# The opening of a two-layer transformer trunk: rows turned ahead of the modulation, its sums split over two engines, weights laid out in slabs by the host, and a written order on three engines

## The chip, the cores and the metric

The kernel runs on one core of one Trainium2 chip. The metric is device time in microseconds (us) of one launch; the median of three runs before the change is 1437.43 us (1436.27 to 1440.77).

In the rows, PE is TensorE (matmuls and transposes), PEld its weight loads, DVE VectorE, ACT ScalarE, POOL GpSimd; SPq is the queue on which SyncE issues most DMAs.

## The reference, cut to what matters

512 rows of 1024 go through two layers. The opening is the first block's modulated norm and its projection to queries and keys:

```python
cond = silu(c)
mod = cond @ ada_w[0] + ada_b[0]                 # (1, 6 * 1024)
sh1, sc1, g1, sh2, sc2, g2 = split(mod, 6)
h = rms_norm(x, norm_mix[0]) * (1 + sc1) + sh1   # (512, 1024)
q, k, v = split(h @ a_w_in, 3)                   # a_w_in: (1024, 3072)
q, k = rms_norm of each head of 64
```

Then come attention with a position bias, the output projection, a squared-ReLU MLP, a second layer with spatial gating in place of attention, and its MLP.

## The kernel before

Every float32 matmul is made of three passes over rounded halves, high by high, high by low and low by high (`mm3`). So each weight tile is split after it is loaded: ScalarE casts the high half, VectorE subtracts for the low half (`wload`, lines 402 and 403; `wload_half`, 854 and 855). Memory is a pool of 49 slots (`SL`), PSUM 8 banks (`bank`).

The opening cuts the 1024 input columns into four chunks of 256. For a chunk, `stage_load` loads eight slab rows of `ada_w` for shift and scale (each 128 x 512, shift and scale side by side) and lets VectorE add them, each times its element of `cs`, into one running sum (line 209). For chunk 0 the shift half goes another way: `shift_first` lets TensorE make the sums, one column of 128 at a time. `stage_mod` sums the partitions by four matmuls of one column, closes shift and scale (lines 893 to 896), turns the normed rows of the chunk's two blocks of 128 by transposes (`turn`, line 902), modulates each block on ScalarE (line 911), and splits it (916, 917). `stage_q0` and `stage_q1` are the chunk's share of the query columns 0 to 511 and 512 to 767: 24 matmuls of 512 columns and 24 of 256. After chunk 3 comes the K block: `gemm_tok(h, k_w, t, ps)` for four tiles of rows, 96 matmuls of 512 columns, which needs all eight blocks of `h`. Its banks are two free ones and then those of the queries, which come free when `qk_norm` (lines 982 to 988) has normed and copied them out. Then the attention heads begin, with the rest of the projection as filler.

Instructions are placed on each engine by a scheduler that works before the run, and each engine then keeps its order. Some stretches are written in order for TensorE by `in_order()`; the opening isn't. `bg` puts the sums of later modulations behind the instruction in `mark`.

Of the kernel before, what the change touches and what calls it, by code (L numbers as in the profile page):

```python
# [52 lines left out]
def trunk_kernel(  # L53
# [37 lines left out]
    def bank():  # L91
        return PS.get([P, 512], F32)
# [41 lines left out]
    ps, i = bank()  # L134
    T.transpose(ps[:, 0:P], vecs, ident)
    V.tensor_copy(vecT, ps[:, 0:P])
    T.transpose(ps[:, P:P + 2], qk2, ident[0:2, 0:2])
    V.tensor_scalar(qkg[:, 0:1], ps[:, P:P + 1], -0.5 * HD ** -0.5, None, ALU.mult)
    V.tensor_scalar(qkg[:, 1:2], ps[:, P + 1:P + 2], -0.5, None, ALU.mult)
    PS.free(i)  # L140
# [38 lines left out]


# [4 lines left out]
    def ada_acc(l, ms, c0, n, box):  # L185
# [5 lines left out]
        def load(k0):  # L191
            box[k0] = raw, done = raw_tile([P, kl, nm * n])
            src = ada_w[l].rearrange("(p k) (m j) -> p k m j", p=P, m=6)[:, k0:k0 + kl, ms[0]:ms[-1] + 1, c0:c0 + n]
            for k in range(kl if nm > 1 else 0):
                SP.dma_start(raw[:, k, :].rearrange("p (m j) -> p m j", m=nm), src[:, k])
            if nm == 1:
                SP.dma_start(raw, src[:, :, 0, :])
# [91 lines left out]
    region = []  # L289

    def in_order():
        region.append(tc.manual_schedule(engines={mybir.EngineType.PE}))
        region[-1].__enter__()
# [99 lines left out]
    def wload(src, nk, k0=0, engs=(V,)):  # L393
# [3 lines left out]
        for k in range(k0, k0 + nk, kp):  # L397
# [7 lines left out]
            w += [(hi[:, o, :], lo[:, o, :]) for o in range(kp)]  # L405
            ids += [i, j]
# [431 lines left out]
    rows = [norm_rows(t, V) for t in range(NT)]  # L838
    SL.free(*xid)
    first = [bank() for t in range(NT)]  # L840
    second = [bank() for _ in range(NT // 2)]
    first_ids = []
    zeros, zi = SL.get([P, 512], F32R)
    G.memset(f32(zeros), 0.0)
    for ps, _ in second:
        mm(ps, ones, zeros, True, False)

    def wload_half(src, k0, nk, eng):

        raw, done = raw_tile([P, nk, 256])  # L850
        loaded[0] = SP.dma_start(raw, src[k0 * P:(k0 + nk) * P, :].rearrange("(k p) n -> p k n", p=P))
        hi, i = SL.get([P, nk, 256], F32R)
        lo, j = SL.get([P, nk, 256], F32R)
        A.copy(hi, raw)
        eng.tensor_tensor(lo, raw, f32(hi), ALU.subtract)
        done()
        first_ids.extend([i, j])
        return [(hi[:, o, :], lo[:, o, :]) for o in range(nk)]

    def shift_first(n):  # L860

        nk, kl = n // P, D // n
        ps, pi = bank()
        mm(ps[:, 0:nk], ones, zeros[:, 0:nk], True, False)
        modT[0, 0] = cp.tile([P, KD], F32, name="mod00")
        for k0 in range(0, KD, kl):
            raw, done = raw_tile([P, kl, n])
            SP.dma_start(raw, ada_w[0].rearrange("(p k) j -> p k j", p=P)[:, k0:k0 + kl, 0:n])
            for k in range(kl):
                for j in range(nk):  # L870
                    mm(
                        ps[:, j:j + 1], raw[:, k, j * P:(j + 1) * P], cs[:, k0 + k:k0 + k + 1],
                        False, k0 + k == KD - 1 and j == nk - 1,
                    )
            done()
        V.tensor_tensor(modT[0, 0][:, 0:nk], ps[:, 0:nk], vecT[:, 0:nk], ALU.add)
        PS.free(pi)

    def mod_columns(c0, n, accs):

        k0, nk = c0 // P, n // P
        ps, pi = bank()
        for i, (m, acc) in enumerate(accs):
            if (0, m) not in modT:
                modT[0, m] = cp.tile([P, KD], F32, name=f"mod0{m}")
            r = modT[0, m][:, k0:k0 + nk]
            for j in range(nk):
                o = i * nk + j
                mm(ps[:, o:o + 1], acc[:, j * P:(j + 1) * P], f32(ones)[:, 0:1], True, True)
            col = m * KD + k0  # L890
            src = ps[:, i * nk:(i + 1) * nk]
            if m == 0:
                V.tensor_tensor(r, src, vecT[:, col:col + nk], ALU.add)
            else:
                V.scalar_tensor_tensor(r, src, 1.0, vecT[:, col:col + nk], ALU.add, ALU.add)
                V.tensor_tensor(r, r, vecT[:, 96 + k0:96 + k0 + nk], ALU.mult)
        PS.free(pi)

    def turn(k):
        ps, pi = bank()  # L900
        for t in range(NT):
            T.transpose(ps[:, t * P:(t + 1) * P], rows[t][0][:, k * P:(k + 1) * P], ident)
        return ps, pi

    split = [None]

    def modulate(turned, k0):
        for o, (ps, pi) in enumerate(turned):
            tt = tp.tile([P, 512], F32, tag="tt", name="tt")
            k = k0 + o  # L910
            A.activation(
                tt, ps, AF.Identity, bias=modT[0, 0][:, k:k + 1], scale=modT[0, 1][:, k:k + 1],
            )
            PS.free(pi)
            hi, lo = h[k]
            split[0] = A.copy(hi, tt)
            mark[0] = V.tensor_tensor(lo, tt, f32(hi), ALU.subtract)

    cw, nk = 256, 2
    state = {}  # L920

    def stage_load(ci):
        c0, k0 = ci * cw, ci * nk
        box = {}
        if ci == 0:
            shift_first(cw)
        for load, use in ada_acc(0, (1,) if ci == 0 else (0, 1), c0, cw, box):
            load()
            use()
        w, ids = wload(a_w_in[0][:, 0:512], nk, k0)  # L930
        first_ids.extend(ids)
        w2 = wload_half(a_w_in[0][:, 512:768], k0, nk, V)
        state[ci] = box, w, w2

    def stage_mod(ci):
        c0, k0 = ci * cw, ci * nk
        box = state[ci][0]
        turned = [turn(k0)]
        ms = (1,) if ci == 0 else (0, 1)
        mod_columns(c0, cw, [(m, box["acc"][:, i * cw:(i + 1) * cw]) for i, m in enumerate(ms)])  # L940
        SL.free(box["id"])
        turned += [turn(k0 + 1)]
        modulate(turned, k0)

    def stage_q0(ci):
        for t in range(NT):
            gemm_tok(h, state[ci][1], t, first[t][0], ci * nk, KD - 1)

    def stage_q1(ci):
        k0 = ci * nk  # L950
        for t in range(NT):
            ps = second[t // 2][0][:, t % 2 * 256:t % 2 * 256 + 256]
            gemm_tok(h, state[ci][2], t, ps, k0, KD - 1 + (t + 1) % 2, False)

    stage_load(0)
    stage_mod(0)
    for ci in range(1, 4):
        stage_load(ci)
        stage_q0(ci - 1)
        stage_mod(ci)  # L960
        stage_q1(ci - 1)
    stage_q0(3)
    stage_q1(3)
    SL.free(zi, *[i for _, i in rows])
    for l, m in ((0, 2), (0, 4), (0, 3), (0, 5), (1, 1), (1, 0), (1, 2), (1, 4), (1, 3), (1, 5)):
        bgq.extend(ada_mod(l, m))

    qk = {}
# [541 lines left out]
```

## Time and profile before

| | us |
|---|---|
| median of three runs | 1437.43 |
| the profiled execution, its own time | 1437.91 |
| its span, first to last instruction | 1436.1 |
| TensorE busy in the span | 1391.4 |
| VectorE, ScalarE busy | 1020.0, 709.1 |
| mean granted TensorE clock, of full speed | 0.988 |

The span is 1.8 us shorter than the time of the same execution. A busy TensorE is not one at its peak: at half the clock it is as busy.

### The profile page before, as it was taken

To read this page: it belongs to the slowest core of one execution; us is meant where nothing else is said; L and a number is where in the kernel's file an instruction comes from. 1 tells how busy PE (TensorE), PEld (TensorE's weight loads), DVE (VectorE), ACT (ScalarE), POOL (GpSimd) and SP (SyncE) were. 2 spreads that over 40 slices of the span, in tenths; PEclk is the share of its full clock that TensorE was granted. 3 is DMA by queue.
4 is the path that set the end of the run, shared out by engine and by line. 5 is a ranking of instruction groups with operands and counts; after the bars stand their busy time and mean duration, and the time that the engine had idled before them with its cause. 6 is when DMAs were issued, how large, how long until landed. Compare 5 with 4: busy or idle time off the path is not lost.

```text
span 1436.1 us, 18871 instructions
## 1 busy us (share of the span) xinstructions
PE 1391.4 (97%) x7186; PEld 1191.1 (83%) x7186; DVE 1020.0 (71%) x1493; ACT 709.1 (49%) x1228; POOL 10.0 (1%) x34
## 2 busy tenths in 40 slices
PE   6989889899999999999999999999999999999998
PEld 5879879779988888888888888788889988888887
DVE  6577899767577877786996754667677366776882
ACT  4426677655454543555677542233346455453630
POOL 0000000000000000000000000000000000000000
PEclk9999999999999999999999999999999999999999
DMA  9736654556236263167133343345337226152141
GB/s 335 242 107 188 195 175 126 184 205 235 73 118 219 75 220 103 38 223 275 66 118 105 123 128 111 114 140 183 103 132 264 76 72 196 54 162 88 30 161 59
DMA packets 95459, 208.93 MB, mean 145 GB/s; under 512 B 7808, under 2 KB 25608, under 8 KB 95368
## 3 DMA queue, kind: packets, MB, share of 16 engines
q1 hardware_dynamic: 95184, 207.66, 44.5%
q8 instruction: 56, 0.92, 0.3%
q14 instruction: 35, 0.29, 0.1%
q10 hardware_dynamic: 184, 0.07, 0.0%
HBM read 190.92 MB, written 8.39 MB: 139 GB/s over the span
## 4 chain that ended last, share of the span: by engine, by line
PE 77%; DMA 2%; DVE 1%; ACT 1%; issue 0%; SPq 0%; DVEq 0%; ACTq 0%
PE p L95 76%; DMA s<-in_ffn_w 1%; DVE s L403 1%; PE p L1421 1%; PE p L329 1%; DMA s<-in_b_w_in 0%; ACT s L480 0%; DMA s<-in_b_w_out 0%; PE p L222 0%; PE p L380 0%; DVE s L481 0%; ACT s L402 0%; ACT tt L333 0%; DVE s L1119 0%; DVE s L1143 0%
## 5 line engine op out<-in xcount | busy, mean ns | idle before, releaser
L95 PE MATMUL p<-s,s 128*128 128x512 f32 (+2 forms) x6568 | 1333.0, 363 | 19.9 <-DVE s L988 4.1
L95 PEld LDWEIGHTS p<-s,s 128*128 128x128 f32 x6568 | 1117.5, 191 | 208.4 <-ACT ry L151 4.5
L481 DVE TENSOR_TENSOR s<-s,s 128x1024 fp32r<-128x1024 f32 x234 | 280.3, 1219 | 113.0 <-ACT s L480 53.7
L480 ACT CAST s<-s 128x1024 fp32r<-128x1024 f32 x234 | 241.6, 1051 | 174.5 <-PE p L95 109.4
L403 DVE TENSOR_TENSOR s<-s,s 128x1024 fp32r<-128x1024 f32 x102 | 123.3, 1221 | 70.5 <-ACT s L402 59.3
L402 ACT CAST s<-s 128x1024 fp32r<-128x1024 f32 x102 | 106.3, 1050 | 114.4 <-DMA s<-in_b_w_in 27.8
L209 DVE SCALAR_TENSOR_TENSOR s<-s,cs,s 128x1024 f32<-128x1024 f32 (+2 forms) x98 | 108.6, 1109 | 12.9 <-DMA s<-in_ada_w 11.8
L628 DVE TENSOR_TENSOR s<-s,s 128x1024 f32<-128x1024 f32 x64 | 77.3, 1219 | 34.1 <-DMA s<-in_ffn_w 30.9
L736 ACT ACTIVATE r<-p 128x512 f32<-128x512 f32 x64 | 38.1, 595 | 116.7 <-PE p L95 116.6
L514 DVE TENSOR_TENSOR s<-p,s 128x512 f32<-128x512 f32 x104 | 70.3, 684 | 34.6 <-PE p L95 33.4
L742 ACT ACTIVATE s<-r 128x256 f32<-128x256 f32 (+1 forms) x112 | 44.9, 443 | 1.2
L421 DVE TENSOR_TENSOR tr<-p,s 128x512 f32<-128x512 f32 (+1 forms) x33 | 21.9, 670 | 30.3 <-PE p L95 30.0
L318 ACT ACTIVATE s<-s 128x512 f32<-128x512 f32 x32 | 20.2, 632 | 37.8 <-DVE s L422 34.8
L1081 ACT ACTIVATE s<-s,nm 128x384 f32<-128x384 f32 (+3 forms) x64 | 35.7, 559 | 6.3 <-DVE nm L1076 4.6
L1402 ACT CAST s<-s 128x512 fp32r<-128x512 f32 x24 | 14.5, 620 | 44.2 <-DVE s L1400 25.6
L1427 DVE TENSOR_TENSOR s<-p,s 128x256 fp32r<-128x256 f32 x48 | 19.8, 416 | 21.8 <-ACT s L1426 21.7
L1398 ACT ACTIVATE s<-p 128x512 f32<-128x512 f32 x24 | 14.3, 598 | 40.8 <-PE p L95 40.6
L1076 DVE CUSTOM_DVE_ANT_0 s<-p,s 128x384 f32<-128x384 f32 (+3 forms) x64 | 28.8, 484 | 7.6 <-PE p L95 6.1
L527 DVE TENSOR_TENSOR s<-s,s 128x1024 f32<-128x1024 f32 x28 | 33.5, 1217 | 1.0 <-PE p L95 0.9
L1119 DVE TENSOR_TENSOR s<-p,s 128x512 fp32r<-128x512 f32 (+3 forms) x64 | 29.2, 481 | 0.9 <-ACT s L1118 0.8
L1114 PE MATMUL p<-ident,s 128*128 128x128 f32 x160 | 24.0, 276 | 5.8 <-ACT sq L1195 3.2
L1426 ACT CAST s<-p 128x256 fp32r<-128x256 f32 x48 | 17.5, 372 | 24.2 <-PE p L1421 17.6
(129 smaller groups left out, 680.4 us busy)
## 6 DMA issues: line engine op xcount, KB each, us to landing
s<-in_ffn_w SPq DMA_DIRECT2D x128, 512.0 KB, 4.6
s<-in_ada_w SPq DMA_DIRECT2D x84, 512.0 KB, 4.5
s<-in_b_w_in SPq DMA_DIRECT2D x48, 512.0 KB, 4.7
s<-in_b_w_out SPq DMA_DIRECT2D x24, 512.0 KB, 4.8
s<-in_a_w_in SPq DMA_DIRECT2D x22, 512.0 KB, 6.5
s<-s SPq DMA_DIRECT2D x64, 128.0 KB, 2.5
s<-in_ada_w SPq DMA_DIRECT2D x24, 256.0 KB, 6.6
s<-in_x SPq DMA_DIRECT2D x8, 512.0 KB, 5.3
```

Source lines behind the costliest of these rows:

```text
L95: T.matmul(ps, lhsT, rhs, start=start, stop=stop, skip_group_check=more)
L209: V.scalar_tensor_tensor(acc, r, ck, acc, ALU.mult, ALU.add)
L402: A.copy(hi, raw)
L403: engs[len(ids) // 2 % len(engs)].tensor_tensor(lo, raw, f32(hi), ALU.subtract)
L480: A.copy(self.hi, raw)
L481: mark[0] = V.tensor_tensor(self.lo, raw, f32(self.hi), ALU.subtract)
L514: V.tensor_tensor(dst, ps, dst, ALU.add)
L527: V.tensor_tensor(self.ab[d][0], self.ab[a][0], self.ab[b][0], o)
L628: V.tensor_tensor(x[0], y_[0], z[0], ALU.subtract)
L736: A.activation(r, ps, AF.Relu)
L742: A.activation(d, v, AF.Square)
L1081: A.activation(pt[it], pt[it], AF.Exp, bias=nm[:, it:it + 1], scale=-1.0, accum_out=sm[:, it:it + 1])
```

## The change

All rows of `x` are normed and turned ahead of the modulation; blocks that wait are copied from their banks into slots (`keep_turned`). The half of the squares of a row goes to VectorE. A chunk's eight slab rows are shared: TensorE takes three of chunk 0 and one of chunk 1 as columns (`column_of`), VectorE the others (`add_part`). The host lays out `ada_w` and `a_w_in` so that a load is one contiguous run of 4 KB (one of 2 KB) per partition. TensorE, VectorE and ScalarE keep the written order from the start of the opening to `any_order()`. 20 matmuls of zeros run first. The mark for the background sums is set on the last query norm.

```diff
 def ada_acc(l, ms, c0, n, box): ... def load(k0):
-            for k in range(kl if nm > 1 else 0):
-                SP.dma_start(raw[:, k, :].rearrange("p (m j) -> p m j", m=nm), src[:, k])
...
+                src = flat(ada_w, (c0 // n * P * KD + k0) * 512, [[KD * 512, P], [1, kl * 512]])
+                SP.dma_start(raw.rearrange("p k n -> p (k n)"), src)
...
+    def wload_slabs(src, offset, count, n, engs=(V,)):
...
+            loaded[0] = SP.dma_start(
+                raw.rearrange("p k n -> p (k n)"), flat(src, offset + s * P * 1024, [[1024, P], [1, 1024]])
+            )
...
-    rows = [norm_rows(t, V) for t in range(NT)]
...
+    in_order(ENG.PE, ENG.DVE, ENG.Activation)
+    u = st.tile([P, 1], F32, tag="ry1", name="ry")
+    A.activation(u, f32(ones)[:, 0:1], AF.Abs_reciprocal_sqrt)
...
+    for i in range(20):
+        mm(sums[0][0], ones, zeros, True, True)
...
+    def norm_sums(t):
...
+        A.activation(nt[:, 0:512], xt[t][:, 0:512], AF.Square, scale=D ** -0.5, accum_out=ss[:, 0:1])
+        V.tensor_tensor_reduce(
+            out=nt[:, 512:D], in0=xt[t][:, 512:D], in1=xt[t][:, 512:D], scale=1.0 / D, scalar=EPS,
+            op0=ALU.mult, op1=ALU.add, accum_out=ss[:, 1:2],
+        )
...
+    def norm_scale(t):
...
+        nt, c = rows[t][0], (D, 0, D, 512)[t]
+        if c:
+            V.tensor_scalar(nt[:, 0:c], xt[t][:, 0:c], u, None, ALU.mult)
+        if c < D:
+            A.activation(nt[:, c:D], xt[t][:, c:D], AF.Copy, scale=u)
...
+    def keep_turned(k):
...
+        A.copy(nT[k // 2][0][:, k % 2, :], ps)
+        PS.free(pi)
...
+    def column(ci, src, right, stop=False):
+        for j in range(4):
+            mm(sums[ci][0][:, j:j + 1], src[:, j * P:(j + 1) * P], right, False, stop and j == 3)
...
+    def add_part(ci, k):
...
+            V.tensor_scalar(box["acc"], r, cs[:, k:k + 1], None, ALU.mult)
+        else:
+            V.scalar_tensor_tensor(box["acc"], r, cs[:, k:k + 1], box["acc"], ALU.mult, ALU.add)
...
+    def end_columns(ci):
+        box = accs[ci][0]
+        column(ci, box["acc"], f32(ones)[:, 0:1], True)
...
+    def mod_close(ci):
...
+        V.scalar_tensor_tensor(sc, ps[:, NC:2 * NC], 1.0, vecT[:, KD + k0:KD + k0 + NC], ALU.add, ALU.add)
+        V.scalar_tensor_tensor(sc, sc, -0.5, vecT[:, 96 + k0:96 + k0 + NC], ALU.mult, ALU.mult)
+        V.tensor_tensor(sh, ps[:, 0:NC], vecT[:, k0:k0 + NC], ALU.add)
...
+    def stage_q(ci, n):
+        for o, (wh, wl) in enumerate(chunks[ci][0][n]):
+            k = ci * NC + o
+            ah, al = h[k]
+            for i, (l, r) in enumerate(((ah, wh), (ah, wl), (al, wh))):
+                for t in range(NT):
...
+    V.tensor_copy(vecT, vps[:, 0:P])
...
+    for k in (2, 3, 4, 5, 7):
+        add_part(0, k)
+    column_of(0, 6)
+    w_load(0)
+    ada_load(1)
+    keep_turned(2)
+    keep_turned(3)
+    end_columns(0)
+    mod_close(0)
+    for high, _ in chunks[0][1]:
+        high()
+    turn((6, 7), range(NT))
...
+    mod_high(0)
+    mod_high(1)
+    for _, low in chunks[0][1]:
+        low()
+    mod_low(0)
+    mod_low(1)
+    for k in range(4, KD):
+        keep_turned(k)
...
+    for k in range(1, KD):
+        add_part(1, k)
+    stage_q(0, 0)
     for ci in range(1, 4):
-        stage_load(ci)
-        stage_q0(ci - 1)
-        stage_mod(ci)
-        stage_q1(ci - 1)
-    stage_q0(3)
-    stage_q1(3)
+        w_load(ci)
+        if ci < 3:
+            ada_load(ci + 1)
+        end_columns(ci)
...
+        stage_q(ci - 1, 1)
+        (h0, l0), (h1, l1) = chunks[ci][1]
+        h0()
+        h1()
+        l0()
+        mod_close(ci)
+        l1()
+        k = ci * NC
+        mod_high(k)
+        mod_high(k + 1)
+        if ci < 3:
...
+            add_part(ci + 1, 0)
+        mod_low(k)
+        if ci < 3:
+            add_part(ci + 1, 1)
+        mod_low(k + 1)
+        for i in range(2, KD if ci < 3 else 0):
+            add_part(ci + 1, i)
+        stage_q(ci, 0)
+    stage_q(3, 1)
+    any_order()
...
-        qk_norm([qk_tile("q", 1, t)[:, 0:256] for t in (2 * b, 2 * b + 1)], second[b][0])
+        mark[0] = qk_norm([qk_tile("q", 1, t)[:, 0:256] for t in (2 * b, 2 * b + 1)], second[b][0])
...
+        if name == "a_w_in":
+            w = a[0].reshape(4, 2, P, 3072).transpose(0, 2, 1, 3)
...
```

`w_load`, `stage_q`, `mod_high` and `mod_low` do for a chunk what `wload` with `wload_half`, the `gemm_tok` of a stage, and `modulate` did; `stage_q` takes the three passes of a block one after another over all four tiles of rows.

Three places of the order. ScalarE at chunk 2, before: L402 and L854 cast chunk weights, but `s24_92` is a filler weight of the attention; L911 and L916 modulate blocks 4 and 5.

```order
L402 CAST s21_57_481<-s19_56_479 128x1024
L854 CAST s20_60_487<-s25_59_485 128x512
L402 CAST s24_92_921<-s23_91_919 128x1024
L911 ACTIVATE tt_426<-p0_15_408,mod00_173,mod01_226 128x512
L916 CAST s8_9_109<-tt_426 128x512
L911 ACTIVATE tt_430<-p7_17_421,mod00_173,mod01_226 128x512
L916 CAST s8_9_109<-tt_430 128x512
```

Now (L890 casts chunk weights, L418 the filler weight, L986 and L991 modulate):

```order
L890 CAST s48_49_444<-s47_48_442 128x1024
L890 CAST s2_52_448<-s1_51_446 128x512
L986 ACTIVATE tt_493<-s33_34_302,mod00_107,mod01_108 128x512
L418 CAST s24_95_944<-s23_94_942 128x1024
L991 CAST s8_9_103<-tt_493 128x512
L986 ACTIVATE tt_496<-s33_34_302,mod00_107,mod01_108 128x512
L991 CAST s8_9_103<-tt_496 128x512
```

The filler's cast stood ahead of both modulations of the chunk; now it stands between the two steps of the first, in an order that ScalarE must keep.

SyncE's queue now, from chunk 3's last slabs on (L195 and L880 load chunk 3; L413 `s23` and `s48` are filler weights, `s39`, `s43`, `s47`, `s21` the K weights; L192 is for background sums):

```order
L195 DMA s15_57_456<-in_ada_w 128x1024
L195 DMA s21_54_450<-in_ada_w 128x1024
L880 DMA s18_62_540<-in_a_w_in 128x512
L880 DMA s22_59_536<-in_a_w_in 128x1024
L413 DMA s23_94_942<-in_a_w_in 128x1024
L413 DMA s39_71_642<-in_a_w_in 128x1024
L413 DMA s43_74_648<-in_a_w_in 128x1024
L192 DMA s38_99_975<-in_ada_w 128x1024
L413 DMA s47_77_654<-in_a_w_in 128x1024
L192 DMA s40_100_978<-in_ada_w 128x1024
L413 DMA s21_80_660<-in_a_w_in 128x1024
L413 DMA s48_102_1031<-in_a_w_in 128x1024
```

The two filler loads stand behind all of chunk 3, and the second one behind the K weights too.

VectorE between chunk 3 and the first query norm, before (L209 with 128x1024 is a background sum, L403 a weight split, L917 the low half of block 6 or 7, L984 the sums of squares of a query tile):

```order
L207 TENSOR_SCALAR s2_81_877<-s25_80_875,cs_79 128x1024
L403 TENSOR_TENSOR s42_70_622<-s39_68_619,s41_69_621 128x1024
L209 SCALAR_TENSOR_TENSOR s2_81_877<-s16_82_879,cs_79,s2_81_877 128x1024
L403 TENSOR_TENSOR s47_73_628<-s43_71_625,s44_72_627 128x1024
L403 TENSOR_TENSOR s3_76_634<-s40_74_631,s1_75_633 128x1024
L209 SCALAR_TENSOR_TENSOR s2_81_877<-s35_96_952,cs_79,s2_81_877 128x1024
L403 TENSOR_TENSOR s19_79_640<-s17_77_637,s18_78_639 128x1024
L984 TENSOR_REDUCE ss8_645<-sq_643 128x8
L984 TENSOR_REDUCE ss8_658<-sq_656 128x8
L403 TENSOR_TENSOR s22_104_1017<-s0_102_1014,s21_103_1016 128x1024
L209 SCALAR_TENSOR_TENSOR s2_81_877<-s37_97_955,cs_79,s2_81_877 128x1024
```

Now (L419 splits weights, L994 is the low half of block 6 or 7, L1111 the sums of squares):

```order
L994 TENSOR_TENSOR s11_12_106<-tt_579,s10_11_105 128x512
L419 TENSOR_TENSOR s2_104_1034<-s48_102_1031,s0_103_1033 128x1024
L994 TENSOR_TENSOR s11_12_106<-tt_582,s10_11_105 128x512
L419 TENSOR_TENSOR s42_73_645<-s39_71_642,s46_72_644 128x1024
L419 TENSOR_TENSOR s45_76_651<-s43_74_648,s44_75_650 128x1024
L419 TENSOR_TENSOR s16_79_657<-s47_77_654,s1_78_656 128x1024
L419 TENSOR_TENSOR s14_82_663<-s21_80_660,s13_81_662 128x1024
L1111 TENSOR_REDUCE ss8_668<-sq_666 128x8
L1111 TENSOR_REDUCE ss8_681<-sq_679 128x8
L419 TENSOR_TENSOR s17_107_1040<-s3_105_1037,s25_106_1039 128x1024
L141 TENSOR_SCALAR ra_670<-ss8_668 128x8
```

The background sums are gone from ahead of the norms, and all four K splits stand ahead of them.

## Rows read from the trace of the kernel before

**Rows 1.** The page: the span, and in its part 1 busy time, share of the span and instructions of each engine.

```profile
span 1436.1 us, 18871 instructions
...
PE 1391.4 (97%) x7186; PEld 1191.1 (83%) x7186; DVE 1020.0 (71%) x1493; ACT 709.1 (49%) x1228; POOL 10.0 (1%) x34
```

**Rows 2.** Busy time by stretch of the first 100 us. Columns: stretch and its length; busy us and number of instructions of PE, PEld (weight loads), DVE, ACT, POOL; mean granted TensorE clock; busy share of the DMA engines; GB/s.

```profile
0.00:24.00 24.00, 12.98 (x54) 11.04 (x54) 14.30 (x38) 12.14 (x29) 1.32 (x8) 1.00 0.97 325
24.00:40.00 16.00, 12.75 (x64) 10.95 (x65) 14.60 (x25) 5.25 (x8) 0.00 (x0) 0.92 1.09 355
40.00:62.00 22.00, 22.00 (x126) 19.44 (x124) 8.87 (x17) 7.39 (x11) 0.00 (x0) 0.90 0.75 262
62.00:82.00 20.00, 19.68 (x97) 16.30 (x96) 18.78 (x26) 12.57 (x21) 0.14 (x1) 1.00 0.46 148
82.00:86.00 4.00, 0.02 (x1) 0.05 (x1) 4.00 (x16) 1.20 (x4) 0.14 (x1) 0.91 0.50 164
86.00:100.00 14.00, 14.00 (x50) 11.24 (x51) 7.71 (x32) 1.16 (x4) 0.15 (x1) 0.78 0.19 64
```

**Rows 3.** The timeline of PE, and one row of that of ACT. Columns: start us, us, engine, line, operation, out<-in, shapes, count; in brackets the idle time before it and who ended it. The first row is the four sums of a chunk by columns; L902 turns rows, L95 is every matmul. The last row starts when the K block of the opening has ended.

```profile
19.47 0.98 PE L95 MATMUL p<-ones,s 128*128 128x1 f32 x4 [1.14 <-DVE s L209]
23.95 7.85 PE L95 MATMUL p<-s,s 128*128 128x512 f32 x29
...
37.60 1.12 PE L902 MATMUL p<-ident,s 128*128 128x128 f32 x4 [2.74 <-DVE mod L895]
...
85.98 14.02 PE L95 MATMUL p<-s,s 128*128 128x512 f32 x48 [4.07 <-DVE s L988]
...
100.04 0.60 ACT L982 ACTIVATE sq<-p 128x512 f32<-128x512 f32 x1 [3.56 <-PE p L95]
```

**Rows 4.** Groups of instructions of DVE from 10 to 62 us, shapes kept apart. Columns: line, engine, operation, names, shapes, count | busy us, mean ns of one | idle time before them and who ended it. L209 adds one slab row of the modulation weights to the running sum, L403 and L855 make the low half of a weight split, L917 that of the modulated rows, L320 scales a tile of rows, L895 closes two columns of the modulation.

```profile
L209 DVE SCALAR_TENSOR_TENSOR s<-s,cs,s 128x512 f32<-128x512 f32 x21 | 15.7, 749 | 0.3
L403 DVE TENSOR_TENSOR s<-s,s 128x1024 fp32r<-128x1024 f32 x5 | 6.1, 1221 | 4.2 <-ACT s L402 4.2
L917 DVE TENSOR_TENSOR s<-tt,s 128x512 fp32r<-128x512 f32 x6 | 4.1, 686 | 2.7 <-ACT s L916 2.7
L320 DVE TENSOR_SCALAR s<-s,ru 128x1024 f32<-128x1024 f32 x4 | 3.0, 748 | 0.0
L855 DVE TENSOR_TENSOR s<-s,s 128x512 fp32r<-128x512 f32 x4 | 2.7, 684 | 0.0
...
L895 DVE SCALAR_TENSOR_TENSOR mod<-p,vecT 128x2 f32<-128x2 f32 x4 | 0.6, 153 | 4.0 <-PE p L95 4.0
```

**Rows 5.** The same of ACT: L402 and L854 make the high half of a weight split, L911 modulates a block of turned rows, L916 makes its high half.

```profile
L402 ACT CAST s<-s 128x1024 fp32r<-128x1024 f32 x5 | 5.2, 1047 | 16.1 <-DMA s<-in_a_w_in 16.1
L911 ACT ACTIVATE tt<-p,mod,mod 128x512 f32<-128x512 f32 x7 | 5.2, 775 | 16.7 <-DVE mod L896 16.4 <-PE p L902 0.4
L916 ACT CAST s<-tt 128x512 fp32r<-128x512 f32 x7 | 4.1, 618 | 0.1
L854 ACT CAST s<-s 128x512 fp32r<-128x512 f32 x4 | 2.5, 614 | 0.0
```

**Rows 6.** The timeline of ACT at the start of the program, with its own DMA issues (ACTq).

```profile
1.67 1.28 ACT L111 ACT_TABLE_LOAD   x1 [1.67 <-PEq L1493]
...
4.02 0.57 ACTq L128 DMA_DIRECT2D qk<-in_a_k_gain  x1
5.00 0.63 ACT L318 ACTIVATE s<-s 128x512 f32<-128x512 f32 x1 [1.83 <-DMA s<-in_x]
```

**Rows 7.** DVE from 100 to 125 us, the group whose operation is of the kind that the change brings into the opening: two inputs, one output and a sum in one pass.

```profile
L1076 DVE CUSTOM_DVE_ANT_0 s<-p,s 128x512 f32<-128x512 f32 x2 | 1.4, 686 | 0.0
```

**Rows 8.** Two stretches of the DMA engines, columns as in rows 2: rows of 4 KB (the tiles of x) from 3 to 8 us, and pieces of 1 KB (`in_ada_w`) with some of 2 KB from 10 to 20 us.

```profile
3.00:8.00 5.00, 0.45 (x1) 0.18 (x1) 0.07 (x1) 3.17 (x10) 0.00 (x0) 1.00 0.98 378
10.00:20.00 10.00, 8.33 (x39) 7.99 (x39) 9.48 (x26) 3.63 (x11) 0.00 (x0) 1.00 1.10 354
```

**Rows 9.** A lone weight transfer, from its issue on SP to the ACT instruction that waited for it; and an ACT row that waited for another such transfer between two modulations.

```profile
69.98 0.38 SPq L399 DMA_DIRECT2D s<-in_a_w_in  x1
...
73.69 1.05 ACT L402 CAST s<-s 128x1024 fp32r<-128x1024 f32 x1 [2.88 <-DMA s<-in_a_w_in]
...
47.53 1.05 ACT L402 CAST s<-s 128x1024 fp32r<-128x1024 f32 x1 [4.03 <-DMA s<-in_a_w_in]
```

**Rows 10.** Stretches of the chunks and of the K block, columns as in rows 2, at the two levels of the granted clock; and a row of the timeline of PE with 48 matmuls of 256 columns.

```profile
38.00:44.00 6.00, 5.49 (x20) 4.42 (x19) 5.93 (x11) 4.04 (x6) 0.00 (x0) 0.50 1.06 379
86.00:92.00 6.00, 6.00 (x14) 4.73 (x15) 5.42 (x25) 0.36 (x2) 0.00 (x0) 0.50 0.06 19
93.00:100.00 7.00, 7.00 (x33) 5.74 (x32) 2.29 (x7) 0.81 (x2) 0.15 (x1) 1.00 0.33 112
...
106.91 5.99 PE L95 MATMUL p<-s,s 128*128 128x256 f32 x48
```

**Rows 11.** Groups of DVE from 62 to 86 us, columns as in rows 4: L209 here adds a background row of 1024, L984 sums the squares of a query or key tile.

```profile
L209 DVE SCALAR_TENSOR_TENSOR s<-s,cs,s 128x1024 f32<-128x1024 f32 x5 | 6.4, 1275 | 0.0
L984 DVE TENSOR_REDUCE ss<-sq 128x8 f32<-128x512 f32 x8 | 5.1, 672 | 0.0
```

**Rows 12.** Two stretches of the attention heads, columns as in rows 2.

```profile
180.00:220.00 40.00, 34.31 (x252) 32.71 (x252) 36.75 (x106) 25.95 (x62) 1.66 (x5) 0.96 0.59 167
220.00:260.00 40.00, 37.83 (x291) 35.27 (x289) 37.04 (x93) 30.26 (x76) 1.05 (x4) 1.00 0.57 152
```

## What is predicted, and why

> **What bounds the kernel now.** I read the page's busy shares first: TensorE is busy for 1391.4 of 1436.1 us [rows 1], so most of the program ends when its matmuls end, and nothing in the change touches them. Then I read the stretches of the first 100 us [rows 2]. TensorE is busy for only 81.4 of them, and 4 us are empty. In the timeline [rows 3] the first large matmul starts at 23.95, a gap of 2.74 us ends at 37.60, one of 4.07 at 85.98, and the K block has ended by 100.0. Three things hold TensorE there. The first modulation is late. Between chunks VectorE is slow: it is busy for 14.6 of the 16 us to 40. And at 82 the third K tile has no bank, because VectorE has not yet normed the queries; it is busy for all 4 us. [...]
>
> So the change is worth the shift of the end of the K block, as long as the attention behind it keeps its length. I build that moment from durations.
>
> **Chunk 0.** ScalarE issues its own DMAs until 4.02 + 0.57 = 4.6; the added table load (1.28, as the other one) and its probe (an estimate of 0.2) follow, so the first half square starts at 6.1 instead of 5.00, and gives its sum at 7.0 [rows 6]. The new two-input square on VectorE isn't in this opening; its nearest row is 0.69 [rows 7], and with a read of its sum I take 0.75; between nothing, where ScalarE sets the pace anyway, and the 1.2 of a 1024 wide operation its three uses leave a range of 2 us. VectorE then does three of them (2.3), twelve one-column steps of 0.15 to 0.2 (2.4), scales two and a half tiles (1.9 by L320), makes three copies (an estimate of 0.6) and adds five slab rows at 0.75 (3.75) [rows 4]. It waits some 1.2 us for ScalarE, which scales a tile (a cast of the same size is 1.05) before it squares tile 3 [rows 5]. That is 19.1. Four columns on TensorE (0.98 [rows 3]) and three closing steps of 0.15 end the modulation at 20.5.
>
> Two blocks are modulated and cast in turn, 2 x (0.78 + 0.62) = 2.8 us [rows 5], and the last bank for the queries is copied out 0.6 later: TensorE starts its 24 matmuls in earnest at 23.9, no earlier than before. In the first such stretch before, 29 matmuls took 7.85 us, which is 3.0 us at 0.43 and the rest at 0.22. I charge the same, although 20 matmuls of zeros run early: TensorE has little to do from about 10 to 21. So 24 matmuls end at 30.7. VectorE is through at 23.3 + 0.7 + 7 x 0.75 = 29.2 with its adds and at 30.5 with the next weight split (1.22). After four columns (0.5 to 1) and the closing, chunk 1 is modulated at 32.0.
>
> **The step from chunk to chunk** is VectorE's: 1.4 until the first block's high half (a small split and the first add hide in it), 0.69 for its low half, an add of 0.75, a low half of 0.69, six adds (4.5), a split (1.22) and the closing (0.45): 9.7 us [rows 4]. TensorE needs 24 x 0.22 + 24 x 0.125 = 8.3 [rows 10], so it is hidden behind VectorE. Sharing the sums changes little from chunk 2 on, where all eight rows are VectorE's. Chunk 2 closes at 41.7.
>
> **The filler weights** are now in that order. On ScalarE a cast of 1.05 stands between the modulation of block 4 and its high half, on VectorE its split of 1.22 ahead of the low half. Block 5, the sums of chunk 3 and the next closing queue up behind them. The transfer is behind 14.4 MB on SyncE's queue: 2.1 of x, 8.4 of `ada_w`, 3.1 of chunk weights, 0.3 of gain and 0.5 of itself. Rows of 4 KB came at 378 GB/s, the mix with 1 KB pieces at 354 [rows 8]. With x done at about 8.4, the remaining 12.3 MB end at 41.0 or 43.2; the cast can start at 41.7 + 0.8 = 42.5, so it waits for nothing or for 0.7. I take nothing, since the slabs are as long as the rows of x.
>
> [...]
>
> The detour makes chunk 3 close 0.78 + 1.05 + 1.22 + 0.69 + 0.75 + 0.69 + 4.5 + 1.22 + 0.45 = 11.35 later, at 53.1. TensorE starts chunk 2 at 41.7 + 0.78 + 1.05 + 0.62 = 44.2 and ends its 512 wide part at 49.5; it then waits 1.9 us for the sums. This end also frees the slot of the second filler weight. Its transfer takes 3.7 us from issue to use, as the lone one did (69.98 to 73.69) [rows 9], and its cast stands ahead of block 6: 49.5 + 3.7 + 1.05 = 54.2, then 1.4 to the high half, 55.6.
>
> **The end.** From 55.6 on TensorE does 24 matmuls and two of K (26 x 0.22 = 5.7), 24 of 256 (3.0) and the other 94 of K (20.7): 85.0. The third K tile needs a bank at 64.3 + 46 x 0.22 = 74.4. VectorE gets to it with two low halves and a split between them (58.2), four K splits (63.1), two sums of squares, two filler splits and four more sums (6.5), about sixteen small steps (2.4) and the norm (0.7): 72.7 [rows 4, 11]. So the 4.07 us go, with 1.7 to spare. Five background sums of 1.28 would put them back; the moved mark keeps these behind the norms. They come later, under the K block, where VectorE is busy for 7.71 of 14 us [rows 2]. The turned rows' copies on ScalarE (six of some 0.6) lie where it waited 16.1 us for weights and 16.4 for sums [rows 5].
>
> 100.0 - 85.0 = 15.0 us. The profiled execution took 1437.91, so 1422.9; the median of the runs is 0.5 lower: **1422.4**.
>
> **The rivals.**
>
> *TensorE stays at the lower level or the bank wait returns.* For it: 2.74 us of gap were followed by 0.50, and my gap is 1.9; the margin at the bank is only 1.7. Against it: the gap is shorter. A fall costs half of 6 us, 3.0; a first stretch all at 0.43 costs 24 x 0.21 = 5.0 less the 1.5 charged; a bank late by 2 brings its 2 and a fall, 5. Two of these give some 6 us back: 1428.
>
> *More is gained.* If no ScalarE wait holds VectorE at the start (1.2), the zeros keep the full level (1.5) and the detours by the filler weights shrink (11.35 to 9.7, and 2.5 at block 6), 7 us come on top: 1415.5. Against it is that strict order.
>
> *The attention gives it back.* It now starts earlier, but its loads and background sums aren't done sooner. From 180 to 260 VectorE is busy for 73.8 of 80 us and TensorE idle for 7.9 [rows 12], and the scheduler writes the heads' order anew. If idle time grows by some 12 us, the gain is 3: 1434.4, no change. Against it: the order of the first heads differs little, and a shift alone makes nothing later relative to TensorE.
>
> *Slower.* The place is the second filler cast. All engines but SyncE must keep their order, so blocks 6 and 7, the K splits and the K block stand behind one transfer, itself behind the K loads on a queue in order. Each us above 3.7 is a us at the end; from 18.7 on nothing is gained, and from 23 the kernel is slower: 1442 at 23. Before, a cast there waited 4.03 us for a transfer [rows 9]. Nothing in the rows comes near 20.
>
> *Without effect* it would be if TensorE's own work set the opening: it doesn't, with 18.6 of 100 us idle [rows 2].
>
> **How the numbers follow.** The forecast has a chance of 0.48, the first rival 0.26, more gained 0.14, given back 0.08, slower 0.04. About 0.3%, 4.3 us, is what a measurement of this kernel can tell from no change. Faster by more needs less than 1433.1: 0.48 + 0.26 + 0.14 and a little of the attention's case, 0.89; the same 0.07; slower 0.04. The range reaches to both middle rivals: below, 1414; above, 1428 and the 2 to 3 us of the unknown square and of the DMA rate, 1431.
>
> **What would show it.** After the change the K block should end near 85, with VectorE busy almost without a break from 24 to 53 and chunk steps of 9.7 and 11.35 us; the first large matmul near 22 to 24; a ScalarE wait for `in_a_w_in` ahead of block 6's modulation, and none of note ahead of block 4's cast; no gap of 4 us at the third K tile; idle time of TensorE after the K block as before. The prediction is wrong if the chunks step at TensorE's 8.3 or by the loads, if the first chunk is done well before 20, or if the attention's idle time moves by more than 5 us.

## The result, and the profile after the change

The changed kernel takes 1426.18 us (median; 1420.26 to 1433.83) against 1437.43 (1435.51 to 1440.77): a ratio of 0.9915, 95% interval 0.9892 to 0.9938, so about 11.3 us faster. Measured once more on another occasion it gave 0.9917 (0.9901 to 0.9934), 1425.3 us. The forecast was 1422.4 with a range of 1414 to 1431.

The page of the changed kernel, as [rows 1]; its profiled execution took 1426.18 us:

```profile
span 1424.2 us, 18890 instructions
...
PE 1391.5 (98%) x7213; PEld 1192.0 (84%) x7213; DVE 1022.2 (72%) x1496; ACT 711.3 (50%) x1229; POOL 9.1 (1%) x34
```

The stretches of [rows 2] and [rows 12] (stretch and length; busy us of PE, PEld, DVE, ACT, POOL; granted clock; DMA share; GB/s):

```profile
0.00:24.00 24.00, 20.16 (x100) 17.89 (x101) 14.02 (x40) 14.65 (x29) 1.32 (x8) 0.84 0.92 354
24.00:40.00 16.00, 16.00 (x84) 13.76 (x83) 13.80 (x22) 6.35 (x10) 0.00 (x0) 0.92 1.03 404
40.00:62.00 22.00, 19.63 (x116) 16.97 (x116) 17.89 (x28) 13.32 (x18) 0.00 (x0) 1.00 0.71 233
62.00:82.00 20.00, 20.00 (x101) 17.02 (x100) 19.45 (x56) 7.43 (x18) 0.14 (x1) 1.00 0.30 104
82.00:86.00 4.00, 4.00 (x19) 3.33 (x18) 3.43 (x7) 0.21 (x1) 0.14 (x1) 1.00 0.75 246
...
180.00:220.00 40.00, 35.91 (x265) 33.40 (x263) 36.99 (x95) 26.23 (x63) 1.60 (x5) 0.96 0.61 177
220.00:260.00 40.00, 34.74 (x221) 31.01 (x220) 31.37 (x79) 27.17 (x68) 1.66 (x5) 0.91 0.64 178
```

The idle 4 us from 82 to 86 of [rows 2] are gone, and the K block runs at a granted clock of 1.00 throughout. TensorE's timeline, against [rows 3]:

```profile
18.38 1.05 PE L95 MATMUL p<-ones,s 128*128 128x1 f32 x8 [0.84 <-DVE s L962]
...
22.56 7.54 PE L95 MATMUL p<-s,s 128*128 128x512 f32 x24
29.94 0.95 PE L95 MATMUL p<-ones,s 128*128 128x1 f32 x8
...
39.75 0.95 PE L95 MATMUL p<-ones,s 128*128 128x1 f32 x8
...
51.11 1.05 PE L95 MATMUL p<-ones,s 128*128 128x1 f32 x8 [1.47 <-DVE s L962]
52.02 3.12 PE L95 MATMUL p<-s,s 128*128 128x256 f32 x24
55.84 30.42 PE L95 MATMUL p<-s,s 128*128 128x512 f32 x144 [0.69 <-ACT s L991]
86.09 0.71 PE L1153 MATMUL p<-ident,s 128*128 128x128 f32 x5
```

and ScalarE's casts of the two filler weights, with the modulation of block 6 behind the second:

```profile
42.28 1.05 ACT L418 CAST s<-s 128x1024 fp32r<-128x1024 f32 x1 [0.27 <-DMA s<-in_a_w_in]
...
53.37 1.05 ACT L418 CAST s<-s 128x1024 fp32r<-128x1024 f32 x1 [6.67 <-DMA s<-in_a_w_in]
54.32 0.81 ACT L986 ACTIVATE tt<-s,mod,mod 128x512 f32<-128x512 f32 x1
```

The K block ends (the first turning of a head, L1025 before, L1153 after) at 86.1 instead of 99.8: 13.7 us. From there to the first turning of the norm behind the heads (L328 and L329) it takes 217.5 instead of 215.0, and from there to the end 1120.6 instead of 1121.3. So 13.7 us are gained in the opening, 2.5 go back in the heads, 0.7 more are gained behind them, and the span is 11.9 us shorter. The heads of the kernel before, of the changed one and of its second execution (e9, below); length, busy us of the engines in the order above, granted clock:

```profile
99.84:314.80 214.96, 196.82 (x1350) 180.50 (x1349) 173.08 (x405) 135.92 (x315) 7.63 (x21) 0.96 0.60 178
86.09:303.57 217.48, 198.56 (x1349) 181.43 (x1348) 174.54 (x408) 136.10 (x315) 6.87 (x22) 0.96 0.60 179
88.37:303.55 215.18, 196.39 (x1349) 179.64 (x1348) 174.22 (x408) 135.96 (x315) 6.77 (x22) 0.97 0.60 180
```

TensorE is idle there for 18.1, 18.9 and 18.8 us. Two executions of one program differ by 2.2 us of busy time, so the 2.5 us are about what the heads vary by themselves.

### The profile page after: what moved, and what is told of

It reads as the page before. It is cut to its first block, busy times and chain, and to the rows that moved or that the text cites. A ratio compares the mean times of both kernels' runs of the same rounds, so it can differ in the third digit from the quotient of the medians.

```text
span 1424.2 us, 18890 instructions
## 1 busy us (share of the span) xinstructions
PE 1391.5 (98%) x7213; PEld 1192.0 (84%) x7213; DVE 1022.2 (72%) x1496; ACT 711.3 (50%) x1229; POOL 9.1 (1%) x34
## 2 busy tenths in 40 slices
DMA packets 82211, 208.94 MB, mean 147 GB/s; under 512 B 7616, under 2 KB 9032, under 8 KB 82120
## 4 chain that ended last, share of the span: by engine, by line
PE 86%; DMA 7%; DVE 4%; ACT 2%; issue 1%; SPq 0%; ACTq 0%; DVEq 0%
PE p L95 84%; DMA s<-in_ada_w 2%; DMA s<-in_a_w_in 1%; DMA s<-in_a_w_out 1%; DMA s<-in_ffn_w 1%; DVE s L207 1%; PE p L1549 1%; PE p L1242 1%; PE p L328 1%; DMA s<-in_b_w_in 0%; ACT s L1209 0%; DVE s L402 0%; DMA s<-in_x 0%; DVE s L1247 0%; DMA s<-s 0%
## 5 line engine op out<-in xcount | busy, mean ns | idle before, releaser
L95 PE MATMUL p<-s,s 128*128 128x512 f32 (+2 forms) x6568 | 1327.6, 362 | 15.5 <-DVE s L1247 3.5
L95 PEld LDWEIGHTS p<-s,s 128*128 128x128 f32 x6568 | 1114.0, 190 | 201.5 <-DVE nm L1204 3.2
L497 DVE TENSOR_TENSOR s<-s,s 128x1024 fp32r<-128x1024 f32 x234 | 280.2, 1219 | 112.4 <-PE p L95 54.2
L496 ACT CAST s<-s 128x1024 fp32r<-128x1024 f32 x234 | 241.7, 1051 | 171.8 <-PE p L95 113.0
L402 DVE TENSOR_TENSOR s<-s,s 128x1024 fp32r<-128x1024 f32 x80 | 96.5, 1219 | 62.2 <-ACT s L401 56.0
L401 ACT CAST s<-s 128x1024 fp32r<-128x1024 f32 x80 | 83.6, 1053 | 86.5 <-DMA s<-in_b_w_in 28.3
L207 DVE SCALAR_TENSOR_TENSOR s<-s,cs,s 128x1024 f32<-128x1024 f32 x70 | 89.6, 1279 | 12.0 <-DMA s<-in_ada_w 11.3
L317 ACT ACTIVATE s<-s 128x512 f32<-128x512 f32 x24 | 15.3, 636 | 34.5 <-DVE s L438 34.5
L1554 ACT CAST s<-p 128x256 fp32r<-128x256 f32 x48 | 17.5, 371 | 24.8 <-PE p L1549 18.3
```

The costliest lines, as they stand in the source:

```text
L95: T.matmul(ps, lhsT, rhs, start=start, stop=stop, skip_group_check=more)
L207: V.scalar_tensor_tensor(acc, r, ck, acc, ALU.mult, ALU.add)
L402: engs[len(ids) // 2 % len(engs)].tensor_tensor(lo, raw, f32(hi), ALU.subtract)
L496: A.copy(self.hi, raw)
L497: mark[0] = V.tensor_tensor(self.lo, raw, f32(self.hi), ALU.subtract)
```

## The experiments

The table gives for each kernel's profiled execution: the start and length of the first 24 large matmuls (29 in the kernel before, to which no such split applies), the end of the K block, the time from there to the norm behind the heads; and the ratio of the times to the kernel before, from all executions.

| kernel | first 24 start, took | K block ends | heads | ratio (95%) |
|---|---|---|---|---|
| before | 23.95, – | 99.8 | 215.0 | 1 |
| changed | 22.56, 7.54 | 86.1 | 217.5 | 0.9915 (0.9892–0.9938) |
| e9, changed again | 24.47, 8.30 | 88.4 | 215.2 | 0.9917 (0.9901–0.9934) |
| e1 late splits | 23.68, 8.12 | 87.4 | 217.2 | 0.9939 (0.9922–0.9957) |
| e2 row shared | 24.92, 7.89 | 91.7 | 214.1 | 0.9953 (0.9933–0.9974) |
| e3 both | 23.57, 7.74 | 88.0 | 219.8 | 0.9945 (0.9924–0.9966) |
| e4 no mark | 23.50, 7.67 | 91.6 | 213.6 | 0.9943 (0.9916–0.9971) |
| e5 mark alone | – | 93.4 | 213.8 | 0.9962 (0.9946–0.9978) |
| e6 no slabs | 23.81, 7.54 | 92.4 | 216.6 | 0.9928 (0.9901–0.9954) |
| e7 no zeros | 25.42, 8.13 | 89.0 | 212.2 | 0.9923 (0.9899–0.9947) |
| e8 TensorE's order alone | 24.42, 8.20 | 87.4 | 215.3 | 0.9931 (0.9913–0.9950) |
| e10 late casts | 23.40, 7.92 | 84.6 | 217.0 | 0.9925 (0.9906–0.9944) |
| e11 more zeros | 22.55, 6.87 | 84.3 | 216.3 | 0.9934 (0.9916–0.9952) |
| e12 zeros and casts | 21.89, 6.88 | 82.6 | 227.3 | 0.9964 (0.9945–0.9983) |

An interval reaches 2 to 4 us to either side, so the times tell e5 and e12 from the changed kernel, e2 just so, and not the rest; what moved in the opening is read from the traces. A profiled execution need not be the typical one: that of e6 was the slowest of five (1432.3 us), that of e10 the fastest of six (1421.4).

**e9: the same kernel again.** No edit.

> The changed kernel once more, unedited, beside the next two on the same chip. Theory A (in the changed kernel the granted clock up to the first 24 large matmuls differs from one execution to the next, which moves the first modulation and so the K block; VectorE's adds of chunk 0 end at 18.3 in every trace): adds again at 18.2 to 18.4, the first modulation closed anywhere from 19.8 to 21.7 and the K block ended from 86 to 89; time 1420 to 1434 from execution to execution. Theory B (the trace after the change shows the opening as it always is): closed at 19.9, the K block ended at 86.1 within 0.3.

Theory A. VectorE's last add of chunk 0 ends at the same time, 18.3, but the K block ends 2.3 us later. The granted clock (the number behind TensorE's count) shows why; the changed kernel first, then e9:

```profile
12.50:16.00 3.50, 3.50 (x20) 0.54 1.03 415
16.00:19.50 3.50, 2.66 (x24) 0.98 1.02 414
19.50:26.00 6.50, 6.50 (x25) 0.51 1.03 407
```

```profile
12.50:16.00 3.50, 3.50 (x21) 0.56 1.02 396
16.00:19.50 3.50, 3.50 (x19) 0.50 1.03 419
19.50:26.00 6.50, 6.50 (x29) 0.50 1.03 409
```

One program, two executions: in the second, TensorE's granted clock stays at 0.50 from 13 us to beyond 26 (0.67 on average from 26 to 32), its turnings and columns are still running when VectorE is through, and the first 24 matmuls start at 24.47 and take 8.30. Every difference of 2 us in the table is read with this in mind, from the start of the 24 to the end of the K block: 63.5 us in the changed kernel, 63.9 in e9.

**e4 and e5: the moved mark, taken away and alone.** The edit of e4; e5 puts the line with `mark[0] =` into the kernel before.

```
-        mark[0] = qk_norm([qk_tile("q", 1, t)[:, 0:256] ...
+        qk_norm([qk_tile("q", 1, t)[:, 0:256] ...
```

> The changed kernel without the moved mark, so the background sums may stand among the query norms again. Theory A (five sums of 1.28 us put VectorE 6.4 us behind, the margin at the bank of the third K tile is about 3.5): a gap of TensorE of 3 us at the third K tile, and a stretch at the lower clock level behind it; the K block ends at 90 to 92, time some 5 us above that of the changed kernel. Theory B (the wait was there only because the modulation was late): no gap, the K block ends at 86, the time is that of the changed kernel.

> The kernel before with the moved mark alone. Theory A (the background sums among the norms made the bank late): the gap of 4.07 us at the third K tile goes, and with it the 6.8 us at the lower clock level (3.4 more), so the K block ends near 93 instead of 100.0, time near 1431. Theory B (the norms are late because the modulation was): a gap of 2 us or more stays, the K block ends at 97 to 100, time 1435 to 1438.

e4, the wait for the bank on TensorE and the norm on VectorE:

```profile
79.10 12.67 PE L95 MATMUL p<-s,s 128*128 128x512 f32 x48 [3.05 <-DVE s L1115]
```

```profile
78.27 1.28 DVE L1115 TENSOR_TENSOR s<-p,ru 128x512 f32<-128x512 f32 x2
```

and in the changed kernel:

```profile
70.26 1.28 DVE L1115 TENSOR_TENSOR s<-p,ru 128x512 f32<-128x512 f32 x2
```

Theory A twice, as to the opening: five adds of 1.28 stand ahead of that norm on VectorE, the gap is 3.05, and the K block ends at 91.6. In e5 the K block runs without a gap and ends at 93.4, and the time is 1430.5 against 1436.8. Alone, one line moves the end of the K block by 6.4 of the 13.7 us, and the time by about half of what the whole change gives. The time of e4 leaves the expected 5 us open: its ratio, 0.9943, is 4 us above the changed kernel's, and the intervals overlap. In the profiled execution the heads took 213.6 instead of 217.5, with 15.2 us of TensorE idle instead of 18.9, so part of what the opening lost came back there.

**e1, e3 and e10: the filler weights.** e1 and e3 wrap the load in `tc.issue_after` on the last query norm; e10 names the last cast of h as well:

```
-            fw[n, cb] = wload_slabs(...)
+            with tc.issue_after(q_done.ins), tc.issue_after(cast_done.ins):
+                fw[n, cb] = wload_slabs(...)
```

> The changed kernel, with the two filler weights' loads, casts and splits held until VectorE has normed the last query tile. Theory A (the detour and the second filler cast cost what the changed kernel's trace shows: 11.4 us for chunk 3's step against 9.9, and 6.67 us of ScalarE idle ahead of block 6): chunk 3 closes near 50.9 instead of 52.6, block 6 follows at once, and the K block ends at 83 to 84 instead of 86.2; time some 2.5 us below that of the changed kernel. Theory B (another thing, VectorE's norms or the K weights, sets the K block as well): its end moves by less than 1 us. Theory C (the weights are then late for the first fillers behind the K block): the K block ends early, but TensorE waits 2 us or more for them, and the time is the same.

> Both: the filler weights held behind the last query norm, and row 0 of chunks 2 and 3 summed on TensorE. Theory A (VectorE paces the chunk steps, the fillers stand in the way): steps of some 9 us, chunk 3 closed at 49.5, the K block ends at 82, and the time is some 4 us below that of the changed kernel, near 1422. Theory B (TensorE's 8.3 us of matmuls and the columns pace them): the K block ends no earlier than with the held fillers alone.

> The changed kernel with the casts of the two filler weights on ScalarE held behind block 7's high half, and their splits on VectorE behind the last query norm (with the splits alone held, the casts stayed where they were and the wait of 6.6 us ahead of block 6 with them). Theory A (the second cast's transfer holds block 6, the first cast and split lengthen chunk 3's step): no cast of 1024 columns ahead of block 6, block 6's modulation begins as soon as chunk 3 is closed, the time from the start of the first 24 large matmuls to the end of the K block, 63.5 us in the changed kernel's trace, falls by 2 to 3.5 us. Theory B (VectorE's or TensorE's other work ends at the same time): it falls by less than 1.

e1 and e3 tested less than meant: held behind a VectorE instruction, VectorE's splits moved; ScalarE's casts stayed in the opening, in e1 with 6.63 us of idle time ahead of the second, which e3 has one place later. From the 24 to the K block's end it is 63.7 in e1 and 64.5 in e3, no gain, and e3's K block ends no earlier than e1's (88.0 and 87.4): its Theory B. In e10 nothing stands ahead of block 6:

```profile
52.20 0.82 ACT L986 ACTIVATE tt<-s,mod,mod 128x512 f32<-128x512 f32 x1 [5.46 <-DVE mod L978]
53.05 0.62 ACT L991 CAST s<-tt 128x512 fp32r<-128x512 f32 x1
```

Chunk 3 closes 9.8 us behind chunk 2 instead of 11.5 (11.1 in e9), and the stretch is 61.2: Theory A, 2.3 to 2.7 us. But behind the K block TensorE waits twice for key norms. VectorE now does three of the held splits from 75.0 to 78.5, and four background adds of 1.28 stand between the last key tile's sum of squares (85.53) and its norm (95.59), in the changed kernel one:

```profile
93.37 0.33 PE L1154 MATMUL p<-ident,s 128*128 128x128 f32 x1 [1.40 <-DVE s L1115]
96.34 0.47 PE L1154 MATMUL p<-ident,s 128*128 128x128 f32 x1 [2.64 <-DVE s L1115]
```

**e2: one row of the sums of chunks 2 and 3 on TensorE.**

```
-            add_part(ci + 1, 0)
+            column_of(ci + 1, 0)
```

> The changed kernel, with row 0 of the sums of chunks 2 and 3 taken from VectorE and put on TensorE as four columns. Theory A (VectorE paces the chunk steps): chunk 2 closes 0.75 us earlier, the slot for the second filler weight comes free 0.75 earlier, so the K block ends about 0.75 earlier, at 85.4. Theory B (TensorE paces them): steps as before or 0.5 longer each, the K block ends at 86.2 to 87.2.

Theory B, and more: 24.92 to 91.7 is 66.8, of which 1.6 is a lower clock in the last 144 matmuls (32.00 us instead of 30.42; granted 0.96 from 62 to 82, not 1.00), behind a wait of 1.78. The closing columns of chunk 2 start 10.71 behind those of chunk 1 (32.65 to 43.36), with no wait of TensorE between; in the changed kernel it is 9.81 (29.94 to 39.75), also with none. TensorE paces that step itself. The next step is 10.71 instead of 11.36: there, with the filler's split on VectorE, the row taken off helps (Theory A), but ScalarE then waits 7.51 us instead of 6.67 for the second filler weight ahead of block 6.

**e6: the slabs undone.** Arrays and loads as before the change.

```
-            SP.dma_start(raw..., flat(a_w_in, off, [[NC * n, P], [1, NC * n]]))
+            SP.dma_start(raw, rows_in.rearrange("(k p) n -> p k n", p=P))
```

> The changed kernel with the arrays and the loads of the kernel before (pieces of 1 to 2 KB instead of rows of 4 KB for each partition), its order of work unchanged. Theory A (12.3 MB at 354 instead of 378 GB/s or more): the first filler weight lands 2 to 3 us later, its cast, which waited 0.27 us, waits that long, and the K block ends 2 to 3 us later, at 88 to 89. Theory B (transfers stay hidden): within 0.5 us of 86.2. Theory C (small pieces hold up the first sums already): the first modulation closes later than 19.9, by 2 us or more, and the K block ends at 91.

```profile
24.00:40.00 16.00, 16.00 (x79) 13.69 (x80) 13.55 (x22) 7.34 (x12) 0.00 (x0) 0.88 1.09 355
```

```profile
45.46 1.04 ACT L399 CAST s<-s 128x1024 fp32r<-128x1024 f32 x1 [2.20 <-DMA s<-in_a_w_in]
...
58.13 1.04 ACT L399 CAST s<-s 128x1024 fp32r<-128x1024 f32 x1 [8.27 <-DMA s<-in_a_w_in]
```

355 GB/s instead of 404. The casts wait 2.20 and 8.27 instead of 0.27 and 6.67, 3.5 us together, as Theory A has it; the first modulation is not late. TensorE's longer gaps (2.15 and 2.28) were followed by slower matmuls besides (24 in 7.36 us where the changed kernel has 5.74, and 144 in 32.01 instead of 30.42; the granted clock is 0.92 from 40 to 62, there 1.00), so the K block ended 6.3 us later than in the changed kernel; from the 24 to its end it is 68.6, 4.7 to 5.1 more than in the two executions of that kernel. The time (0.9928) does not show it.

**e7: without the twenty zeros; e11: with 24 more.**

```
+    column_of(0, 1)
+    warm(vps, 10)    # matmuls of zeros, 256 columns
```

> The changed kernel without the twenty early matmuls of zeros. Theory A (they give nothing, since the first 24 large matmuls ran at the lower level until 26.4 all the same): the K block ends at 86 within 0.5 us. Theory B (without them TensorE reaches the full level later, as at 27.3 in the kernel before, and the transposes and columns go at half speed): the first modulation closes up to 1 us later, the first 24 matmuls take 8 to 10 us instead of 7.5, and the K block ends 1 to 3 us later.

> The changed kernel with 24 more matmuls of zeros (256 columns each) on TensorE between 10 and 19 us, in its waits among the transposes and the columns of chunk 0; nothing else is moved. [...] Theory B (the level falls in spite of them, and each one costs 0.11 to 0.22 us on the way): the K block ends 1 to 4 us later.

Without them the six first turnings take 1.52 instead of 0.84 us and the first 24 start at 25.42, later than in any trace with the zeros. The K block ends 2.9 us later than in the changed kernel's first trace, as Theory B has it, but only 0.6 later than in e9: one trace doesn't tell that from the spread between executions. With more of them (e11):

```profile
12.50:16.00 3.50, 3.50 (x20) 0.56 1.04 410
16.00:19.50 3.50, 3.50 (x32) 0.95 1.03 409
19.50:26.00 6.50, 5.71 (x38) 1.00 1.03 406
```

The level still falls near 13 us, but is back from 16.5 on, and 24 matmuls end 6.87 us after they start, a wait of 0.64 included. The K block ends at 84.3 and not, as in Theory B, 1 to 4 us later than in the changed kernel. How much of that is the clock stays open: in this build the scheduler also moved the filler casts, the first behind the high half of block 5, the second behind that of block 6.

**e8: only TensorE's order written.** `in_order()` instead of `in_order(ENG.PE, ENG.DVE, ENG.Activation)`.

> The changed kernel with only TensorE's order written out; VectorE's and ScalarE's order is the scheduler's. It puts the second filler's cast and split behind blocks 6 and 7, and the first filler's cast behind block 5's high half, while it starts on all four tiles' norms at once. Theory A (the written order costs by the filler detour): chunk 3 closes 1 to 2 us earlier, ScalarE has no 6 us of idle time ahead of block 6, and the K block ends at 83 to 85. Theory B (the written order is what brings the first modulation forward): the first modulation closes 1 us or more after 19.9, chunk steps are longer, and the K block ends at 88 or later.

The stretch from the 24 to the K block's end is 63.0, and the 24 start at 24.42, as in e9 (24.47). Neither theory: the second filler's cast is gone from ahead of block 6, but chunk 3 still closes 11.3 us behind chunk 2. The order written out for VectorE and ScalarE is worth nothing that these traces show.

**e12: both, with the splits where the K splits are.**

```
+    low_done, high_done = mark[0], split[0]      # block 7's halves
...
+            with tc.issue_after(low_done.ins), tc.issue_after(high_done.ins):
```

> The changed kernel with both: 18 more matmuls of zeros (4 and 6 in the first two places, 8 in the third), and the two filler weights' casts held behind block 7's high half, their splits behind its low half (so not behind the query norms, where they put TensorE 4 us into waits for the K norms behind the K block). Theory A (the two effects add, and nothing behind the K block takes them back): the granted clock stays up, chunk steps of 9.8, the first 24 large matmuls start by 22.5, the K block ends at 82 to 83, TensorE's idle time from 82 to 100 stays near 1 us, time 1421 to 1423. Theory B (VectorE's queue behind the opening sets the first heads whatever TensorE does): the K block ends at 82 to 83, but the waits behind it grow by as much, and the time is that of the changed kernel, 1425 to 1426.

The opening does all that Theory A says: first 24 at 21.89, chunk steps of 9.8, K block at 82.6. And it is the slowest variant of the changed kernel, 1430.9, so Theory B has the waits but not their price. The wait behind the K block, and TensorE's busy time and clock there, of e12 and then of the changed kernel:

```profile
93.81 0.33 PE L1163 MATMUL p<-ident,s 128*128 128x128 f32 x1 [3.99 <-DVE s L1124]
```

```profile
82.00:100.00 18.00, 14.01 (x102) 0.91 0.46 135
100.00:180.00 80.00, 73.90 (x558) 0.98 0.58 168
180.00:260.00 80.00, 69.65 (x488) 0.91 0.62 173
260.00:310.00 50.00, 45.36 (x213) 0.93 0.55 187
```

```profile
82.00:100.00 18.00, 16.95 (x125) 1.00 0.56 170
100.00:180.00 80.00, 76.05 (x581) 0.98 0.62 177
180.00:260.00 80.00, 70.65 (x483) 0.94 0.62 177
260.00:310.00 50.00, 45.43 (x217) 0.97 0.55 190
```

The last key norm came at 93.06 (VectorE, L1124), though the K block ended 3.5 us earlier; in the changed kernel it came at 93.70. From the last key tile's sum of squares to that norm it takes 9.5 us, in the changed kernel 6.0: three background adds of 1.28 stand between, not one, and VectorE waits 1.57 for ScalarE, which had a filler weight to cast. That points at the order in these queues. The gap of 3.99 gives back what was gained, and more idle time and lower clock follow up to 310: in all 25.1 us idle in the heads instead of 18.9, and 3.7 more busy. That the new order of the heads causes these later losses is likely, but not shown by a run of its own.

None of the variants beats the changed kernel by more than the measurement can tell. No run takes back the turning ahead of the modulation or the sharing of chunk 0's sums, so how the rest of the 13.7 us divides among the parts of the change is not shown.

## Why the prediction came out as it did

**The bank and the mark** were right: no gap, no fall of the clock (1.00 from 62 to 86), and e5 prices it at 6.4 us. The margin was mis-sized: VectorE frees the bank at 70.9, not 72.7, for a need near 75.3 and not 74.4, so 4.4 us and not 1.7.

**Chunk 0** was forecast to put TensorE's 24 matmuls at 23.9. In seven traces with an untouched opening (the changed kernel, e1 to e4, e9, e10) they start at 22.56 to 24.92, 23.7 on average. That the average is the forecast is partly luck, since what sets it is not what I had on the path. VectorE is through with chunk 0 near 18.3 instead of 19.1, and then waits 1.15 us in the first trace and up to 3.3 in others for TensorE's closing columns, in the others at the lower level (1.84 to 1.87 us instead of 1.05; granted 0.50 from 16 to 19.5 in e9). From there TensorE's own turnings and columns, at the lower level too (0.51 from 19.5 to 26, in e9 0.50), run up to the 24 without a wait, where the sum had ScalarE's modulations and a copy. The 24 take 7.5 to 8.3 us, not the 6.8 of the sum, so this term is short by 0.7 to 1.5; the rival's "first stretch all at 0.43" would be 10.3. The sum's 0.43 and 0.22 us for a matmul of 512 columns are the paces of the K block before, from 86 to 92 and from 93 to 100 us, at a granted clock of 0.50, the lower level, and of 1.00 [rows 10].

**The chunk steps** of 9.7 and 11.35 measured 9.8 and 11.5, from closing to closing, but the first for another reason. TensorE's 8.3 left out the columns (0.95), the zeros that open two banks (0.72) and the open of the next sums; with them it needs 9.81 and waits for nothing. "Hidden behind VectorE" failed: the engines tie (VectorE's last add of chunk 2 ends at 39.5, TensorE begins its closing columns at 39.75), and a row moved to TensorE makes the step longer (e2).

**The filler weights**: the first cast waited 0.27 (0 to 0.7 forecast), the second stood at 53.37 (53.2), 3.7 us after its load was issued at 49.67 as forecast, and held block 6 as predicted; block 6's high half was done at 55.7 (55.6). e10 prices this detour at 2.3 to 2.7 us.

**The end**: from there 144 matmuls took 30.4 us, not 29.4, since one of 512 columns costs 0.228 (30.42 less 3.0 for the 24 of 256, over 120) and not 0.22: 1.0 short. Together 85.0 became 86.1 in one execution and 88.4 in another.

**The heads** kept their length within 2.5 us, and TensorE's idle time in them within 0.8, so the rival in which idle time grows and gives the gain back did not come about. Of the forecast's miss of 3 to 4 us, 1.1 lies in the opening and 2.5 in the heads of the profiled execution, 3.4 and 0.2 in e9's, and some 0.7 comes off behind the heads in both. In the first the 1.1 is the matmul's price, and its early start was used up before block 6; in e9 the later start (0.6) and the slower first burst (1.5) come on top of that price.

**The rivals.** "More is gained" rested on three things, and none came: VectorE waited 1.28 us for ScalarE at 12.3, the level fell at 12.8 in spite of the zeros (0.54 from 12.5 to 16), and both detours by the filler weights stayed. The slow case needed a transfer of 23 us; it took 3.7, and the longest wait for one was 8.3, without the slabs.

## What to carry to other kernels

Price an engine's step with all that stands in its queue, the small matmuls too, before calling it hidden. A gain at the front of a scheduled program needn't reach its end, since the edit can change the order behind it: e12 gained 3.5 us more in the opening, and its time was 5 to 7 us longer. And look where the first falls of the clock stand before reading 2 us out of a single trace.

## What the runs showed of the hardware

TensorE's granted clock fell to 0.50 near 12.8 us in the changed kernel, behind waits of 0.97 and 0.42 us, and stayed there until 16 although the engine was busy all through, with turnings and matmuls of one column. In e9 such work kept it busy from 11.6 us to the first large matmul at 24.47, and from 13 on the level was 0.50 throughout. With matmuls of zeros between these it was 0.95 from 16 to 19.5 and 1.00 from there to 32 in e11, and 1.00 from 24 to 40 in e12, where eight one-column matmuls took 0.95 us from 17.1 on; the changed kernel without them had 1.00 from 16.5 to 19 as well, and 0.50 again from 20 on, behind a wait of 0.84. So the zeros may keep the level up, but two traces don't show it apart from chance. A row's 1.00 need not be the pace of its stretch: in e7 the rows show it from 6 to 26 us, while eight one-column matmuls take 1.85 us there and 0.95 later.

With rows of 4 KB the DMA engines moved 399 to 406 GB/s from 24 to 40 us, in eleven traces, with pieces of 1 to 2 KB 354 to 355, in three; the sum had 378. In e6 and the changed kernel the bytes of the whole program are the same (208.94 MB).
